# A triangular inverse by doubling: the level mask put on the product by VectorE, instead of on the matrix by GpSimd

## The chip, the cores and the metric

The kernel runs on one core of one Trainium2 chip. The metric is the time of one execution on the device in microseconds. Five engines work side by side and wait for each other by semaphores: TensorE (PE in the profile; PEld is its loading of weights), VectorE (DVE), ScalarE (ACT), GpSimd (POOL) and SyncE (SP), which issues the DMAs. Matrix products go to PSUM, all other tiles are in SBUF.

## What is computed

One layer over 1024 tokens of width 1024: an RMS norm, one input projection, two mixers side by side (a pooling group and a gated delta rule with four heads), an output projection, a squared-ReLU MLP of width 4096, a final norm. What the change touches is inside the delta rule, where for each chunk of tokens and each head a unit lower triangular system is solved:

```python
    kb = kh * beta[..., None]
    m = jnp.einsum('bhncd,bhnjd->bhncj', kb, kh) * decay_strict
    lhs = jnp.eye(C, dtype=f32) + m
    rhs = jnp.concatenate([vh * beta[..., None], kb * jnp.exp(gcum)[..., None]], axis=-1)
    sol = lax.linalg.triangular_solve(lhs, rhs, left_side=True, lower=True)
```

The kernel takes chunks of 128 tokens, eight in all, and forms the inverse of `lhs` for all four heads of a chunk at a time.

## The kernel before

The tokens are done in two halves of 512. `dense()` is the main thread of TensorE: for each half the projections to k, q, v, z and the pooling input, each in two blocks of 256 columns, then the output projection. Full-precision products are made of three fp32r products of a high and a low part. The parts of the weights come from `split_w` (L125): a load into `raw`, a ScalarE copy to the high part (L132), and a subtraction for the low part `wl` (L133), on VectorE or on GpSimd as the caller says: GpSimd for the k weights of the first half and for all of the second half. A projection to q, k or v ends in `conv_silu` (L378), where VectorE adds three convolution taps to `cy` (L391); the pooling input goes to `pool_group` (L395), a ladder of VectorE additions and small copies `nxt` (L409, L410).

Beside this run "strands", generators that put their instructions between the matmuls of `dense()`. For each chunk `c` there are `prepare` (L510), `query` (L554), `invert` (L573), `correct` (L605) and `scan` (L636). TensorE's order is written out: a counter of matmul time decides which strand puts its next piece after which matmul, and a strand says with `yield` how much TensorE time it leaves before its next piece (`SLACK` is 2.0 us). The orders of VectorE, ScalarE and GpSimd are made by a scheduler when the kernel is built. Each engine works through its order strictly in turn.

`prepare` makes the normalised keys: GpSimd raises the sums of squares `rk` to the power -1/2 (L152), VectorE multiplies (`kn`, L533). Then it makes `m1`, the f16 matrix of all four heads with the identity added (L550), with its rounding rest in `m2` (L549, GpSimd), and GpSimd makes `dec`, `ds` and `kd` (L525, L527, L540). `invert` doubles the size of the inverted diagonal blocks six times, from 2 to 128. `t` is the inverse so far, `tt` its transpose. Before the loop VectorE masks `m1` to the first level (`bl`, L578) and adds the identity (`tt`, L579). In each of the six rounds:

- GpSimd masks `m1` with the constant matrix `lev[l]`, which is -1 in the blocks of that level and 0 elsewhere, into the f16 tile `bl` (L588), one instruction of 128x512 for all heads; `bl` has two buffers.
- TensorE forms the product `px` of `bl` and `t` (L590), four matmuls of 128x128, into a PSUM bank.
- VectorE adds the identity and writes the f16 tile `xx` (L592).
- After 2 us of TensorE time, TensorE forms `tt` times `xx` and `xx` times `tt`, and ScalarE copies both to the new `t` and `tt` (L598, L599).

The seven matrices `lev[l]` are made once at the start by GpSimd (L255 to L260), between its first weight splits.

Of the kernel before, what the change touches and what calls it, by code (L numbers as in the profile page):

```python
# [10 lines left out]
F16 = mybir.dt.float16  # L11
AF = mybir.ActivationFunctionType
ALU = mybir.AluOpType
PSUM = bass.MemoryType.PSUM

P = 128
# [12 lines left out]
def hybrid_trunk(ctx, tc, x, norm_mix, w_in, conv_w, w_pool, pool_scale, a_log, dt_bias,  # L29
                 gdn_norm, w_out, norm_mlp, w_up, w_down, norm_final, out):  # L30
    nc = tc.nc
    V, A, G, T = nc.vector, nc.scalar, nc.gpsimd, nc.tensor
# [54 lines left out]
    ident = const.tile([P, P], F32, name="ident")  # L87
# [153 lines left out]
    ident_h = gp.tile([P, P], F16, name="ident_h")  # L241
# [4 lines left out]
    upto_r = gp.tile([P, P], F32R, name="upto_r")  # L246
    V.tensor_copy(upto_r, upto)

    lev = []
    for l in range(7):  # L250
        b = 1 << l
        m = gp.tile([P, P], F16, name=f"lev{l}")
        nb = P // (2 * b)
        m3 = m.rearrange("p (n q) -> p n q", q=2 * b)
        G.memset(m3[:, :, 0:b], 0.0)  # L255
        G.memset(m3[:, :, b:2 * b], -1.0)

        G.affine_select(m3, m3, pattern=[[-2 * b, nb], [0, 2 * b]], compare_op=ALU.is_ge, fill=0.0, base=0,
                        channel_multiplier=1)
        G.affine_select(m3, m3, pattern=[[2 * b, nb], [0, 2 * b]], compare_op=ALU.is_gt, fill=0.0, base=b,  # L260
                        channel_multiplier=-1)
        lev.append(m)

    cnt_i = gp.tile([P, 16], mybir.dt.int32, name="cnt_i")
# [14 lines left out]
    def done(name, after=0.0):  # L279
        flags[name] = T.now + after  # L280
# [198 lines left out]
    def bc(m):  # L479
        return m.unsqueeze(1).broadcast_to(hs)  # L480
# [7 lines left out]
    def gt(nm, bufs=1, dt=F32, shape=hs, tag=None):  # L488
        return gp.tile(shape, dt, name=nm, tag=tag or nm, bufs=bufs)

    def bank():
        return work_bank().rearrange("p (h c) -> p h c", h=NH)

    def mm(acc, lhsT, rhs, start=True, stop=True):
        for h in range(NH):
            T.matmul(acc[:, h, :], lhsT[:, h, :], rhs[:, h, :], start=start, stop=stop)
# [76 lines left out]
    def invert(c, r):  # L573

        m1 = r["m1"]
        t, tt = gt("t", 3, F16), gt("tt", 3, F16)
        b0 = gt("bl", 2, F16)
        V.tensor_tensor(b0, m1, bc(lev[0]), op=ALU.mult)  # L578
        V.tensor_tensor(tt, b0, bc(ident_h), op=ALU.add)  # L579
        yield 1.0 * SLACK  # L580
        pt = bank()
        for h in range(NH):
            T.matmul(pt[:, h, :], tt[:, h, :], ident_h, start=True, stop=True)
        A.copy(t, pt)
        yield 0.9 * SLACK
        for l in range(1, 7):
            bl = gt("bl", 2, F16)
            G.tensor_tensor(bl, m1, bc(lev[l]), op=ALU.mult)  # L588
            px = bank()
            mm(px, bl, t)  # L590
            xx = gt("xx", dt=F16)
            V.tensor_tensor(xx, px, bc(ident), op=ALU.add)  # L592
            yield 1.0 * SLACK
            pt, ptt = bank(), bank()
            mm(pt, tt, xx)
            mm(ptt, xx, tt)
            t, tt = gt("t", 3, F16), gt("tt", 3, F16)
            A.copy(t, pt)  # L598
            A.copy(tt, ptt)  # L599
            if l < 6:  # L600
                yield 1.0 * SLACK
        r.update(t=t, tt=tt)
        done(f"inverted{c}", 1.0 * SLACK)
# [103 lines left out]
    def inverts():  # L707
        for c in range(NT):
            yield f"prepared{c}"
            yield from invert(c, made[c])  # L710
# [308 lines left out]
    first = {}  # L1019
# [168 lines left out]
```

## Time and profile before

| | |
|---|---|
| median of 3 runs | 1172.87 us (1172.27 to 1178.7) |
| the profiled execution | 1173.46 us, its span in the trace 1171.7 us |
| 0 to 455 us: both halves' projections, with the delta rule beside them | PE busy 415.16, DVE 354.29, ACT 276.09, POOL 214.74 us |
| 455 to 600 us: the rest of the output projection, into the MLP | PE busy 126.50, DVE 96.99, ACT 75.35, POOL 43.53 us |
| 600 us to the end: the MLP and the final norm | PE busy 558.18, DVE 335.27, ACT 251.33, POOL 68.82 us |
| the six masks of a round on GpSimd, L588 | 48 instructions, 62.0 us, 79.9 to 440.6 us |
| the identity added to the product on VectorE, L592 | 48 instructions, 32.8 us |

The profile is of one execution. A row of the timeline has the start, the time taken, the engine, the line, the operation and the tiles as out<-in; in brackets stands how long the engine had been idle before it and what ended that. A row of the waits has the engine that waited, what it waited for, the total in us, the number of times, and the longest. A row of a line's instructions has min/median/max in ns.

### The profile page before, as it was taken

How to read it: one execution, taken by the hardware profiler on the slowest of the kernel's cores; microseconds unless marked ns; L12 is line 12 of the kernel's file. 1: busy time of each engine (PE TensorE's matmuls, PEld its weight loads, DVE VectorE, ACT ScalarE, POOL GpSimd, SP SyncE). 2: the span in 40 equal slices, each digit the busy share in tenths (PEclk: the TensorE clock that was granted, in tenths of full speed). 3: DMA queues.
4: the chain of work that ended last, by engine and by line, in shares of the span. 5: the costliest groups of instructions: out<-in, count | busy, mean ns of one | idle time of the engine just before them, and what ended most of it. 6: DMA issues, size and time to landing. Idle time of an engine off the chain costs nothing.

```text
span 1171.7 us, 15587 instructions
## 1 busy us (share of the span) xinstructions
PE 1099.8 (94%) x5606; PEld 893.7 (76%) x5606; DVE 786.6 (67%) x1224; ACT 602.8 (51%) x1117; POOL 327.1 (28%) x288
## 2 busy tenths in 40 slices
PE   6998999988898999995999999999979999999997
PEld 5777777767687788773788888888868888888886
DVE  5698698878879775559646454545455597465584
ACT  6666566566565554635545454545443333334353
POOL 7033365465754431045132323131100000000010
PEclk9999999999999999997999999999989999999999
DMA  5233211111213321121344444444298797256561
GB/s 161 81 101 116 61 52 41 55 55 43 66 41 126 109 72 37 37 72 54 133 155 153 147 150 152 145 153 145 81 361 294 262 394 242 90 195 192 189 215 72
DMA packets 93047, 155.23 MB, mean 132 GB/s; under 512 B 7781, under 2 KB 45738, under 8 KB 92970
## 3 DMA queue, kind: packets, MB, share of 16 engines
q1 hardware_dynamic: 92970, 154.24, 39.1%
q8 instruction: 44, 0.72, 0.2%
q14 instruction: 33, 0.27, 0.1%
HBM read 120.66 MB, written 33.55 MB: 132 GB/s over the span
## 4 chain that ended last, share of the span: by engine, by line
PE 71%; DVE 12%; ACT 3%; issue 2%; POOL 2%; DMA 0%; POOLq 0%; DVEq 0%; ACTq 0%; SPq 0%
PE bank L44 53%; PE acc L44 17%; DVE cy L391 2%; DVE tl L927 1%; DVE nxt L410 1%; DVE xx L592 1%; PE bank L48 1%; DVE nxt L409 0%; DMA x<-hd 0%; DVE r L918 0%; ACT th L172 0%; DVE ul L173 0%; DVE ml L764 0%; DVE m L546 0%; DVE kn L533 0%
## 5 line engine op out<-in xcount | busy, mean ns | idle before, releaser
L44 PE MATMUL bank<-th,wh 128*128 128x512 f32 x448 | 178.3, 398 | 11.7 <-ACT th L926 10.7
L44 PE MATMUL bank<-tl,wh 128*128 128x512 f32 x448 | 178.1, 398 | 3.0 <-DVE tl L927 2.9
L44 PE MATMUL bank<-th,wl 128*128 128x512 f32 x448 | 177.5, 396 | 2.2 <-DVE wl L933 2.2
L932 ACT CAST sh<-x 128x1024 fp32r<-128x1024 f32 x55 | 57.9, 1054 | 160.9 <-PE bank L44 154.2
L44 PE MATMUL bank<-th,sh 128*128 128x512 f32 x344 | 133.8, 389 | 0.0
L44 PE MATMUL bank<-th,sl 128*128 128x512 f32 x344 | 133.8, 389 | 0.0
L44 PE MATMUL bank<-tl,sh 128*128 128x512 f32 x344 | 133.8, 389 | 0.0
L44 PE MATMUL acc<-uh,wh 128*128 128x512 f32 x320 | 130.4, 407 | 1.1 <-DVE ul L173 0.6
L44 PE MATMUL acc<-ul,wh 128*128 128x512 f32 x320 | 129.3, 404 | 0.0
L932 ACT CAST wh<-wu 128x512 fp32r<-128x512 f32 x112 | 69.1, 621 | 116.0 <-PE bank L44 98.2
L44 PE MATMUL acc<-uh,wl 128*128 128x512 f32 x320 | 128.8, 402 | 0.0
L933 DVE TENSOR_TENSOR sl<-x,sh 128x1024 fp32r<-128x1024 f32 x55 | 67.3, 1223 | 88.1 <-ACT sh L932 88.0
L933 DVE TENSOR_TENSOR wl<-wu,wh 128x512 fp32r<-128x512 f32 x112 | 80.4, 722 | 45.0 <-ACT wh L932 45.0
L44 PEld LDWEIGHTS bank<-th,wh 128*128 128x128 f32 x448 | 85.1, 190 | 32.0 <-ACT th L926 11.4
L44 PEld LDWEIGHTS bank<-tl,wh 128*128 128x128 f32 x448 | 85.0, 190 | 24.5 <-DVE tl L927 5.4
L44 PEld LDWEIGHTS bank<-th,wl 128*128 128x128 f32 x448 | 85.1, 190 | 22.3 <-DVE wl L933 3.1
L152 POOL TENSOR_TENSOR stf<-stf,mhalf 128x1 f32<-128x1 f32 x8 | 7.9, 998 | 329.7 <-DVE stf L1125 329.7
L588 POOL TENSOR_TENSOR bl<-m,lev 128x512 f16<-128x512 f16 x48 | 62.0, 1291 | 82.5 <-PE bank L44 70.2
L391 DVE SCALAR_TENSOR_TENSOR cy<-cr,cols,cy 128x512 f32<-128x512 f32 x72 | 74.1, 1034 | 8.2 <-ACT cy L389 7.7
L133 POOL TENSOR_TENSOR wl<-raw,wh 128x512 fp32r<-128x512 f32 x48 | 68.0, 1421 | 36.4 <-ACT wh L132 36.2
L44 PEld LDWEIGHTS bank<-th,sl 128*128 128x128 f32 x344 | 64.6, 188 | 13.5
L44 PEld LDWEIGHTS bank<-th,sh 128*128 128x128 f32 x344 | 64.6, 188 | 13.5
(325 smaller groups left out, 2372.1 us busy)
## 6 DMA issues: line engine op xcount, KB each, us to landing
w<-in_w_down_dram SPq DMA_DIRECT2D x72, 512.0 KB, 6.9
x<-hd SPq DMA_DIRECT2D x56, 512.0 KB, 3.3
raw<-in_w_in_dram SPq DMA_DIRECT2D x80, 256.0 KB, 2.7
wu<-in_w_up_dram SPq DMA_DIRECT2D x16, 1024.0 KB, 5.4
hd<-s SPq DMA_DIRECT2D x48, 256.0 KB, 2.0
hd<-u SPq DMA_DIRECT2D x32, 256.0 KB, 2.1
raw<-in_w_out_dram SPq DMA_DIRECT2D x24, 256.0 KB, 2.8
xin<-in_x_dram SPq DMA_DIRECT2D x8, 512.0 KB, 5.1
```

Source lines behind the costliest of these rows:

```text
L44: T0.matmul(out, lhsT, rhs, start=start, stop=stop, skip_group_check=goes_on)
L48: T0.transpose(out, in_, identity)
L133: eng.tensor_tensor(lo, raw, hi.bitcast(F32), op=ALU.subtract)
L152: last["rsqrt"] = G.tensor_tensor(s, s, mhalf[:, :n], op=ALU.pow)
L391: V.scalar_tensor_tensor(cy, cr[:, e:e + HALF], tap[e], cy, op0=ALU.mult, op1=ALU.add)
L410: V.tensor_tensor(nxt[:, n:], cur[:, n:], cur[:, :W - n], op=ALU.add)
L588: G.tensor_tensor(bl, m1, bc(lev[l]), op=ALU.mult)
L592: V.tensor_tensor(xx, px, bc(ident), op=ALU.add)
L927: V.tensor_tensor(TL[i][:, j, :], block(r, j), TH[i][:, j, :].bitcast(F32), op=ALU.subtract)
L932: A.copy(hi, src)
L933: V.tensor_tensor(lo, src, hi.bitcast(F32), op=ALU.subtract)
```

## The change

The mask moves from the matrix to the product. Since the mask only selects blocks of the result of `px`, the product of the whole `m1` with `t` can be masked after it. The diagonal of that product is 1 (both factors are unit triangular), so a mask that is 1 on the diagonal puts the identity there as well, and no addition is left. The constants `lev[l]` for l > 0 are laid out transposed and get a diagonal of ones by a third AFFINE_SELECT each; `lev[0]` gets the diagonal too, and `tt` comes of one product.

```diff
@@ in the constants
-        G.memset(m3[:, :, 0:b], 0.0)
-        G.memset(m3[:, :, b:2 * b], -1.0)
-
-        G.affine_select(m3, m3, pattern=[[-2 * b, nb], [0, 2 * b]], compare_op=ALU.is_ge, fill=0.0, base=0,
+        first = l > 0
+        G.memset(m3[:, :, 0:b], -1.0 if first else 0.0)
+        G.memset(m3[:, :, b:2 * b], 0.0 if first else -1.0)
+
+        o = b if first else 0
+        G.affine_select(m3, m3, pattern=[[-2 * b, nb], [0, 2 * b]], compare_op=ALU.is_ge, fill=0.0, base=-o,
                         channel_multiplier=1)
-        G.affine_select(m3, m3, pattern=[[2 * b, nb], [0, 2 * b]], compare_op=ALU.is_gt, fill=0.0, base=b,
+        G.affine_select(m3, m3, pattern=[[2 * b, nb], [0, 2 * b]], compare_op=ALU.is_gt, fill=0.0, base=o + b,
                         channel_multiplier=-1)
+
+        G.affine_select(m, m, pattern=[[-1, P]], compare_op=ALU.not_equal, fill=1.0, base=0, channel_multiplier=1)
         lev.append(m)
@@ invert
-        b0 = gt("bl", 2, F16)
-        V.tensor_tensor(b0, m1, bc(lev[0]), op=ALU.mult)
-        V.tensor_tensor(tt, b0, bc(ident_h), op=ALU.add)
+        V.tensor_tensor(tt, m1, bc(lev[0]), op=ALU.mult)
...
         for l in range(1, 7):
-            bl = gt("bl", 2, F16)
-            G.tensor_tensor(bl, m1, bc(lev[l]), op=ALU.mult)
             px = bank()
-            mm(px, bl, t)
+            mm(px, m1, t)
             xx = gt("xx", dt=F16)
-            V.tensor_tensor(xx, px, bc(ident), op=ALU.add)
+            V.tensor_tensor(xx, px, bc(lev[l]), op=ALU.mult)
```

TensorE's order stays the same, with `m1` as the weights of 192 matmuls where `bl` was. The orders that the scheduler makes change. Lines behind the constants have numbers up to 5 higher in the changed kernel.

VectorE at the first inverse, from the finished `m1` (here `m_816`) to the first `xx`, before:

```order
L550 TENSOR_TENSOR m_816<-m_816,ident_h 128x512
L386 COPY chalo<-cr 128x3
L578 TENSOR_TENSOR bl<-m_816,lev_239 128x512
L391 SCALAR_TENSOR_TENSOR cy<-cr,cols,cy 128x512
L579 TENSOR_TENSOR tt<-bl,ident_h 128x512
L133 TENSOR_TENSOR wl<-raw,wh 128x512
L391 SCALAR_TENSOR_TENSOR cy<-cr,cols,cy 128x512
```

The same place now (`m1` is `m_837`):

```order
L555 TENSOR_TENSOR m_837<-m_837,ident_h 128x512
L391 COPY chalo<-cr 128x3
L584 TENSOR_TENSOR tt<-m_837,lev_239 128x512
L396 SCALAR_TENSOR_TENSOR cy<-cr,cols,cy 128x512
L133 TENSOR_TENSOR wl<-raw,wh 128x512
L396 SCALAR_TENSOR_TENSOR cy<-cr,cols,cy 128x512
```

`bl` is gone, and `tt` stands ahead of the convolution tap that it followed.

GpSimd where the trace of before has 192 to 205 us, from the power of one chunk's output sums (`so`, L152) through the last mask of an inverse to the `kd` of the next chunk, before:

```order
L152 TENSOR_TENSOR so<-so,mhalf 128x4
L525 TENSOR_TENSOR dec<-dec,upto 128x512
L588 TENSOR_TENSOR bl<-m_1817,lev_269 128x512
L133 TENSOR_TENSOR wl<-raw,wh 128x512
L527 TENSOR_TENSOR ds<-dec,ident 128x512
L152 TENSOR_TENSOR rk<-rk,mhalf 128x4
L756 TENSOR_TENSOR qT<-qT,zT 128x4x128
L133 TENSOR_TENSOR wl<-raw,wh 128x512
L540 TENSOR_TENSOR kd<-kn,kds_526 128x512
```

Now:

```order
L152 TENSOR_TENSOR so<-so,mhalf 128x4
L530 TENSOR_TENSOR dec<-dec,upto 128x512
L133 TENSOR_TENSOR wl<-raw,wh 128x512
L532 TENSOR_TENSOR ds<-dec,ident 128x512
L152 TENSOR_TENSOR rk<-rk,mhalf 128x4
L759 TENSOR_TENSOR qT<-qT,zT 128x4x128
L545 TENSOR_TENSOR kd<-kn,kds_547 128x512
```

The mask is gone from the front of `rk`, and a weight split has moved from ahead of `kd` to behind it.

VectorE at the same time, from one `xx` of that inverse to the next and the `kn` of the next chunk, before:

```order
L592 TENSOR_TENSOR xx<-bank,ident 128x512
L530 TENSOR_SCALAR rk<-rk 128x4
L391 SCALAR_TENSOR_TENSOR cy<-cr,cols,cy 128x512
L592 TENSOR_TENSOR xx<-bank,ident 128x512
L533 TENSOR_TENSOR kn<-bank,rk 128x512
```

Now:

```order
L595 TENSOR_TENSOR xx<-bank,lev_271 128x512
L535 TENSOR_SCALAR rk<-rk 128x4
L538 TENSOR_TENSOR kn<-bank,rk 128x512
L396 SCALAR_TENSOR_TENSOR cy<-cr,cols,cy 128x512
L595 TENSOR_TENSOR xx<-bank,lev_279 128x512
```

`kn`, which takes the `rk` that GpSimd has worked on, stands ahead of a tap and of the second `xx`. In three other chunks it moves ahead of other work in the same way.

## The prediction

> **What bounds the kernel now.** I read the busy shares of the page first, then the busy times by stretch, then who waits for whom.
>
> ```profile
> PE 1099.8 (94%) x5606; PEld 893.7 (76%) x5606; DVE 786.6 (67%) x1224; ACT 602.8 (51%) x1117; POOL 327.1 (28%) x288
> ...
> 75.00:455.00 380.00, 350.62 (x2299) 283.52 (x2298) 302.08 (x562) 229.17 (x524) 188.07 (x144) 0.99 0.23 71
> ```
>
> PE is busy for 94% of the span. The second line is the stretch from 75 to 455 us, in which the inverses run beside the projections (its columns: length, busy time of PE, PEld, DVE, ACT, POOL, granted clock, DMA share, GB/s). PE is busy for 350.62 of 380 us. PE's order is written by hand and the change leaves it alone, so nothing but PE's idle time in this stretch, 29.4 us, and matmuls at a lower clock can be won here. Who ends that idle time:
>
> ```profile
> POOL bl L588 <- PE bank L44: 70.2, 20, 7.9
> ...
> PE bank L44 <- DVE xx L592: 15.1, 10, 3.0
> PE bank L48 <- DVE kn L533: 2.9, 2, 1.5
> PE acc L44 <- DVE wol L133: 2.9, 1, 2.9
> PE bank L44 <- DVE nxt L409: 1.7, 1, 1.7
> ...
> PE bank L48 <- DVE on L679: 0.8, 1, 0.8
> ```
>
> PE hardly ever waits for GpSimd's masked matrices: GpSimd waits 70.2 us for PE before it makes them. PE waits for **VectorE**: 15.1 + 2.9 + 2.9 + 1.7 + 0.8, and 0.7 for tt, shown below, are 24.1 us (waits under 0.8 us are left out). So the removal of bl is worth nothing as a shorter path. It is worth what GpSimd does to VectorE meanwhile:
>
> ```profile
> L391 DVE SCALAR_TENSOR_TENSOR cy<-cr,cols,cy x72: 734/752/1846, 27.2 to 313.4; 128x512 f32<-128x512 f32 x72
> L592 DVE TENSOR_TENSOR xx<-bank,ident x48: 673/682/693, 89.5 to 451.3; 128x512 f16<-128x512 f32 x48
> ```
>
> (min/median/max in ns.) The convolution tap, with two inputs in SBUF, takes 752 ns as a rule and up to 1846; xx, with one input in PSUM, never over 693. The long ones stand beside GpSimd instructions, as the next rows show.
>
> **The change part by part.** *First place, the first inverse.* VectorE, then GpSimd, then PE:
>
> ```profile
> 79.81 0.42 DVE L578 TENSOR_TENSOR bl<-m,lev 128x512 f16<-128x512 f16 x1
> 80.15 1.65 DVE L391 SCALAR_TENSOR_TENSOR cy<-cr,cols,cy 128x512 f32<-128x512 f32 x1
> ...
> 82.67 1.63 DVE L391 SCALAR_TENSOR_TENSOR cy<-cr,cols,cy 128x512 f32<-128x512 f32 x1
> ...
> 84.90 2.31 DVE L391 SCALAR_TENSOR_TENSOR cy<-cr,cols,cy 128x512 f32<-128x512 f32 x2
> 79.86 1.40 POOL L588 TENSOR_TENSOR bl<-m,lev 128x512 f16<-128x512 f16 x1 [0.54 <-DVE chalo L386]
> 82.22 1.54 POOL L588 TENSOR_TENSOR bl<-m,lev 128x512 f16<-128x512 f16 x1 [0.96 <-DVE tt L579]
> 85.06 1.61 POOL L588 TENSOR_TENSOR bl<-m,lev 128x512 f16<-128x512 f16 x1 [1.30 <-PE bank L44]
> 82.20 0.40 PE L44 MATMUL bank<-ident_h,tt 128*128 128x128 f16 x4 [0.74 <-DVE tt L579]
> 90.25 0.52 PE L44 MATMUL bank<-xx,tt 128*128 128x128 f16 x4 [2.97 <-DVE xx L592]
> ```
>
> Three times a bl runs and the tap beside it ends with it: 1.65 - 0.75 = 0.90, 1.63 - 0.75 = 0.88 and 2.31 - 2 x 0.75 = 0.81 us. With bl gone these 2.59 us go, and the 0.42 us of L578, whose work (mask, then identity) is one product now. So tt takes the place of L578 at 79.81, ahead of the tap, and PE's 0.74 us go; xx, behind the same taps and the same `at` as before, comes about 3.0 us earlier, and PE, itself 0.74 us earlier, finds it some 0.7 us late instead of 2.97. Of 3.71 us, 3.0 go.
>
> *Second place, a middle inverse:*
>
> ```profile
> 367.51 1.27 DVE L764 TENSOR_TENSOR ml<-pT,mh 128x512 fp32r<-128x512 f32 x1
> ...
> 370.83 0.68 DVE L764 TENSOR_TENSOR ml<-pT,mh 128x512 fp32r<-128x512 f32 x1
> 371.43 1.65 DVE L764 TENSOR_TENSOR ml<-qT,mh 128x512 fp32r<-128x512 f32 x1
> 367.06 1.17 POOL L588 TENSOR_TENSOR bl<-m,lev 128x512 f16<-128x512 f16 x1 [0.36 <-DVE tt L579]
> ...
> 371.12 1.41 POOL L588 TENSOR_TENSOR bl<-m,lev 128x512 f16<-128x512 f16 x1 [0.77 <-PE bank L44]
> 375.44 0.40 PE L44 MATMUL bank<-xx,tt 128*128 128x128 f16 x4 [1.43 <-DVE xx L592]
> ```
>
> Against the unhindered 0.68 us of a split, 0.59 + 0.97 us are lost beside bl, and an L578 goes too (0.42): more than the 1.43 us that PE waits. All 1.43 go.
>
> *Third place, where no bl is near:*
>
> ```profile
> 356.79 1.25 DVE L409 COPY nxt<-nxt 128x4 f32<-128x4 f32 x1
> 356.71 1.30 POOL L133 TENSOR_TENSOR wl<-raw,wh 128x512 fp32r<-128x512 f32 x1 [1.81 <-ACT wh L132]
> 361.04 0.38 PE L44 MATMUL bank<-xx,tt 128*128 128x128 f16 x4 [2.50 <-DVE xx L592]
> ```
>
> Here a copy of four columns takes 1.25 us beside one of GpSimd's weight splits, and the splits stay. Nothing of the 2.50 us goes.
>
> Together the three places hold 3.71 + 1.43 + 2.50 = 7.64 us of waits, and 3.0 + 1.43 = 4.43 go: 58%. I carry that share over to all: 0.58 x 24.1 = 14.0 us. Where PE stops waiting it meets the next VectorE result sooner; I let a third come back as new waits, a choice between none and half, and keep 9.3 us. Against that third also stands a change of order: at one place xx comes behind a third tap where it had two ahead of it, at 0.75 us unless the queue is empty.
>
> *The clock.* Windows of 4 us, granted clock third from the end:
>
> ```profile
> 90.00:94.00 4.00, 3.75 (x16) 3.07 (x16) 2.21 (x5) 2.11 (x4) 0.00 (x0) 0.57 0.68 268
> 322.00:326.00 4.00, 4.00 (x21) 3.55 (x22) 2.18 (x7) 1.63 (x3) 1.16 (x1) 0.57 0.00 0
> 362.00:366.00 4.00, 4.00 (x25) 3.09 (x24) 3.97 (x10) 3.89 (x10) 1.87 (x2) 1.00 0.94 360
> ```
>
> Twice the clock falls after a pause, at (1 - 0.57) x 4 = 1.7 us each; after the 2.50 us pause at 358 it does not. The first fall follows the 2.97 us wait, which I expect gone: 1.7 us more. The other I leave. The Trainium skill (TensorE: Matmul & The Clock Gate, Why this matters for your kernels) warns only of idle gaps above about 3 us; by that the pause of 2.97 us would cost nothing, the term would be nought and the time 1.7 us longer. The rows show the drop, and decide.
>
> *The prices of the instructions.*
>
> ```profile
> L588 POOL TENSOR_TENSOR bl<-m,lev 128x512 f16<-128x512 f16 x48 | 62.0, 1291 | 82.5 <-PE bank L44 70.2
> L619 DVE TENSOR_TENSOR hh<-bank,tt x8: 673/680/692, 129.1 to 459.5; 128x512 f16<-128x512 f32 x8
> L579 DVE TENSOR_TENSOR tt<-bl,ident_h x8: 409/411/1269, 81.7 to 416.0; 128x512 f16<-128x512 f16 x8
> L260 POOL TENSOR_SCALAR_AFFINE_SELECT lev<-lev x7: 294/400/704, 18.7 to 25.9; 128x128 f16<-128x128 f16 x7
> 26.59 3.00 POOL L133 TENSOR_TENSOR wl<-raw,wh 128x512 fp32r<-128x512 f32 x2 [0.38 <-ACT wh L132]
> ```
>
> The 48 xx multiply a PSUM bank by an f16 mask where they added an f32 identity. The nearest row is hh, a PSUM bank with an f16 tile: 680 ns against 682, so nothing; at worst 48 x (693 - 682) ns = 0.5 us, at best 0.4 the other way. The new tt is an f16 product as L578 is: 0.41 us, and up to 1.27 beside GpSimd. The seven added AFFINE_SELECT cost GpSimd 7 x 0.40 = 2.8 us (2.1 to 4.9). They go among the first weight splits, of which the last ends at 29.59; they are hidden by the weights that PE still has, since no wait of PE is ended by GpSimd, and I cost them at nothing. If that cover failed, the last two splits would be up to 4.9 us late. The dense m1 in the place of bl as PE's weights changes no count of loads or matmuls: nothing.
>
> The sum: 9.3 + 1.7 = 11.0 us off the profiled execution's own 1173.46 us gives **1162 us**; the median of the runs shown, 1172.87, is 0.6 us lower.
>
> **The rivals.** *The collisions only move.* GpSimd's splits, no longer queued behind bl, start earlier and hold VectorE elsewhere, as at 358. For it: they and the other GpSimd work are 188.07 - 62.0 = 126 us of the stretch. Against it: nothing refills the 62. The Trainium skill (SBUF — State Buffer, Who interferes with whom) says that of a VectorE instruction with two SBUF inputs and a GpSimd instruction that reads SBUF, the second blocks until the first ends; the rows at 80 to 85 us agree (0.81 to 0.90 us each). By that rule alone bl could hold VectorE for up to 62.0 us, far over what PE waits, and as many collisions as splits would remain. Time if nine tenths come back: 0.1 x 14.0 = 1.4 us, 1172 us; with the noise 1168 to 1174.
>
> *Full relief.* VectorE's load falls, from 302.08 of 380 us, so far that its queue empties between inverses: three quarters of the 24.1 us and both falls of the clock go, 18.1 + 3.4 = 21.5 us: 1152 us.
>
> *Slower: kn ahead of its turn.* In the new VectorE order kn, which waits for GpSimd's rk, stands in four chunks ahead of work that it followed, once ahead of a tap and of xx:
>
> ```profile
> 196.61 1.17 POOL L588 TENSOR_TENSOR bl<-m,lev 128x512 f16<-128x512 f16 x1
> ...
> 200.22 1.01 POOL L152 TENSOR_TENSOR rk<-rk,mhalf 128x4 f32<-128x4 f32 x1
> 200.72 0.75 DVE L391 SCALAR_TENSOR_TENSOR cy<-cr,cols,cy 128x512 f32<-128x512 f32 x1 [2.92 <-ACT cy L389]
> ```
>
> VectorE's queue is in order, so tap and xx wait behind kn. Without bl, rk ends at about 201.23 - 1.17 = 200.06, before the tap could start at 200.72: free. Should rk end after that, each of the four places costs up to rk and a split ahead of it, about 1.0 + 1.3 = 2.3 us, 9 us in all, and if the relief above fails too the time is 1182 us. It decides from rk later than the tap.
>
> *The change not doing what it says* is out: in the new order of GpSimd no bl is left.
>
> **How the numbers follow.** Forecast 0.58 (1156 with no give-back and the second fall of the clock gone too: 14.0 + 3.4 = 17.4 us; 1166 with half of the 14.0 given back and no fall gone), full relief 0.12, moved collisions 0.23, slower 0.07. Half a per cent, 5.9 us, is about what a measurement of this kernel tells from no change. Faster has forecast and full relief, 0.70; same 0.23; slower 0.07. The range, 1151 to 1173, takes in full relief and the moved collisions and leaves out the slower case and the edges.
>
> **What would show it.** PE's waits for xx in the inverse stretch down from 15.1 to 6 to 8 us; the tap's mean there, with stretched ones only beside splits; the wait at 87 us under 1 us and the clock at 1.00 behind it; the wait at 358 still there; xx at 0.68 us; no PE wait before 50 us that GpSimd ends. I am wrong if VectorE's busy time falls by 25 us or so and PE's waits do not, or if a wait for kn grows.

## The result, and the profile after

| | before | after |
|---|---|---|
| median | 1172.59 us (1172.27 to 1178.7, 4 runs) | 1155.43 us (1154.56 to 1156.41, 4 runs) |
| the profiled execution | 1173.46 us, span 1171.7 us | 1154.56 us, span 1152.9 us |
| mean granted clock of TensorE | 0.984 | 0.987 |

The ratio of the two is 0.9842, with a 95% interval of 0.9818 to 0.9865: 1.6% faster, 17.2 us by the medians. The time is 6.6 us under the forecast 1162 and inside the range.

To see where the 18.8 us between the two spans lie, the same piece of TensorE's program is cut out of both traces. It begins at 75 us and ends at the first transposition of the MLP's input `xn`, which both traces have 2440 matmuls later. The window of before, then that of after (length, busy time of PE, PEld, DVE, ACT, POOL, granted clock, DMA share, GB/s):

```profile
75.00:480.16 405.16, 375.79 (x2440) 304.65 (x2439) 313.42 (x587) 236.91 (x543) 190.19 (x147) 0.99 0.22 67
```

```profile
75.00:462.55 387.55, 371.67 (x2440) 302.56 (x2439) 285.88 (x579) 236.13 (x543) 128.82 (x99) 0.99 0.24 72
```

The piece is 17.6 us shorter; the remaining 1.2 us lie behind it. PE's idle time, length less busy time, fell from 29.4 to 15.9 us: **13.5 us**. Its busy time fell by 4.1 us, and a part of that is the clock, shown below. GpSimd lost 61.4 us and VectorE 27.5 us of busy time. Only about 3.4 us of VectorE's are instructions that are gone (eight of 0.42 us); in the other 24 us the instructions that stayed took less time. The rows below trace that to holds: an instruction is held when it takes longer than alone because a GpSimd instruction is running.

PE's waits in that piece after the change (who waited for what, total, times, longest):

```profile
PE bank L44 <- DVE xx L595: 3.3, 6, 0.8
PE acc L44 <- DVE wol L133: 3.0, 2, 1.9
PE bank L48 <- DVE kn L538: 2.7, 2, 1.4
PE bank L44 <- DVE ee L617: 1.6, 2, 0.9
PE bank L44 <- ACT t L601: 1.6, 3, 1.0
PE bank L44 <- ACT qT L397: 1.5, 1, 1.5
PE bank L44 <- ACT ph L433: 1.1, 1, 1.1
PE bank L48 <- DVE on L682: 0.4, 1, 0.4
```

Of the six waits for VectorE that the forecast summed to 24.1 us, 3.3 + 3.0 + 2.7 + 0.4 = 9.4 are left; those for `nxt` and `tt` are gone. That is 14.7 us, 61%. Against it stand 0.9 us more for `ee`, 0.8 us more for ScalarE's `ph`, 0.4 us more for ScalarE's `t` and `vT`, and 1.5 us for ScalarE's `qT`, a new wait: 3.6 us. Waits of before that the sum had left out are gone too: `y` (1.0 us), `ul` (0.8) and `zT` (0.3).

The two instructions of VectorE that were shown before, now (min/median/max in ns):

```profile
L396 DVE SCALAR_TENSOR_TENSOR cy<-cr,cols,cy x72: 736/746/1872, 27.6 to 300.3; 128x512 f32<-128x512 f32 x72
...
L595 DVE TENSOR_TENSOR xx<-bank,lev x48: 673/684/692, 86.4 to 433.7; 128x512 f16<-128x512 f32 x48
```

The tap's group in 75 to 455 us of the changed kernel (count, then busy us and mean ns), and the same group before:

```profile
L396 DVE SCALAR_TENSOR_TENSOR cy<-cr,cols,cy 128x512 f32<-128x512 f32 x48 | 44.1, 921 | 4.1 <-ACT cy L394 3.6
```

```profile
L391 DVE SCALAR_TENSOR_TENSOR cy<-cr,cols,cy 128x512 f32<-128x512 f32 x48 | 53.9, 1127 | 6.7 <-ACT cy L389 6.3
```

The product costs what the addition did, 684 ns against 682. The tap's mean fell from 1127 to 921 ns, while its longest in this stretch is 1767 ns against 1846 (the 1872 above lies ahead of 75 us): there are fewer collisions, and those that are left are about as long.

The first of the three places of the prediction, after the change; VectorE, then PE, and GpSimd has no row between 79.3 and 90 us:

```profile
79.75 0.42 DVE L584 TENSOR_TENSOR tt<-m,lev 128x512 f16<-128x512 f16 x1
80.09 0.74 DVE L396 SCALAR_TENSOR_TENSOR cy<-cr,cols,cy 128x512 f32<-128x512 f32 x1
...
82.62 0.74 DVE L396 SCALAR_TENSOR_TENSOR cy<-cr,cols,cy 128x512 f32<-128x512 f32 x1
...
86.40 0.68 DVE L595 TENSOR_TENSOR xx<-bank,lev 128x512 f16<-128x512 f32 x1
...
87.13 0.38 PE L44 MATMUL bank<-xx,tt 128*128 128x128 f16 x4 [0.84 <-DVE xx L595]
```

No tap is stretched; PE does not wait for `tt` at all, and 0.84 us for `xx` where it waited 2.97.

The third place, where the forecast left the whole wait of 2.50 us. Before, a second copy was stretched beside the next split, behind the copy at 356.79 that the prediction shows:

```profile
358.67 1.11 DVE L409 COPY nxt<-nxt 128x8 f32<-128x8 f32 x1
358.38 1.38 POOL L133 TENSOR_TENSOR wl<-raw,wh 128x512 fp32r<-128x512 f32 x1 [0.38 <-ACT wh L132]
```

The same place in the changed kernel:

```profile
340.69 1.14 DVE L414 COPY nxt<-nxt 128x8 f32<-128x8 f32 x1
341.74 0.69 DVE L415 TENSOR_TENSOR nxt<-nxt 128x520 f32<-128x520 f32 x1
342.35 0.68 DVE L595 TENSOR_TENSOR xx<-bank,lev 128x512 f16<-128x512 f32 x1
340.49 1.32 POOL L133 TENSOR_TENSOR wl<-raw,wh 128x512 fp32r<-128x512 f32 x1 [3.26 <-ACT wh L132]
342.12 1.44 POOL L133 TENSOR_TENSOR wl<-raw,wh 128x512 fp32r<-128x512 f32 x1 [0.32 <-ACT wh L132]
343.08 0.38 PE L44 MATMUL bank<-xx,tt 128*128 128x128 f16 x4 [0.81 <-DVE xx L595]
```

The two splits are still there, and so is the collision, but one copy is stretched where two were: when the second split begins, at 342.12, VectorE is already at the last addition of the ladder, and the next instruction is `xx`. Its one tensor input of that size is in PSUM; it takes 0.68 us beside the split, so it is not held.

The clock, in windows of 4 us (it stands third from the end of a row), after the change:

```profile
87.00:91.00 4.00, 3.87 (x28) 3.24 (x28) 2.61 (x6) 3.45 (x9) 0.71 (x1) 1.00 0.91 329
...
380.00:384.00 4.00, 2.40 (x10) 1.61 (x11) 3.61 (x7) 0.92 (x2) 1.89 (x2) 0.71 0.24 79
384.00:388.00 4.00, 4.00 (x19) 3.34 (x18) 1.95 (x4) 1.73 (x4) 0.91 (x1) 0.50 0.38 122
```

And before, at the corresponding place of the output projection:

```profile
400.00:404.00 4.00, 3.60 (x12) 2.83 (x13) 3.37 (x7) 1.39 (x3) 1.76 (x2) 0.62 0.36 131
404.00:408.00 4.00, 4.00 (x27) 3.16 (x26) 2.19 (x4) 1.56 (x3) 1.04 (x1) 0.95 0.20 70
```

The falls at 90 and at 322 us are both gone: after the change no window of 4 us between 64 and 380 us is under 1.00. A third one, at 401 us, which the forecast had not listed, has become twice as long. Over the whole span the clock cost (1 - 0.984) x 1171.7 = 18.7 us before and (1 - 0.987) x 1152.9 = 15.0 us after, 3.7 us less.

### The profile page after: what moved, and what is told of

The parts are those of the page before. It is cut to its first block, busy times and chain, and to the rows that moved or that the text cites. A ratio compares the mean times of both kernels' runs of the same rounds, so it can differ in the third digit from the quotient of the medians.

```text
span 1152.9 us, 15516 instructions
## 1 busy us (share of the span) xinstructions
PE 1094.7 (95%) x5606; PEld 890.2 (77%) x5606; DVE 760.5 (66%) x1216; ACT 601.5 (52%) x1117; POOL 267.3 (23%) x247
## 4 chain that ended last, share of the span: by engine, by line
PE 73%; DVE 9%; ACT 3%; POOL 2%; issue 2%; DMA 1%; POOLq 0%; DVEq 0%; SPq 0%; ACTq 0%
PE bank L44 54%; PE acc L44 18%; DVE cy L396 2%; DVE tl L930 1%; PE bank L48 1%; POOL rk L152 1%; DVE xx L595 0%; DMA x<-hd 0%; ACT th L172 0%; DVE r L921 0%; POOL wl L133 0%; DVE nxt L415 0%; DVE wl L936 0%; DVE m L551 0%; POOL wu L955 0%
## 5 line engine op out<-in xcount | busy, mean ns | idle before, releaser
L44 PE MATMUL bank<-th,wh 128*128 128x512 f32 x448 | 178.2, 398 | 11.5 <-ACT th L929 10.5
L44 PEld LDWEIGHTS bank<-th,wh 128*128 128x128 f32 x448 | 85.1, 190 | 31.8 <-ACT th L929 11.2
L152 POOL TENSOR_TENSOR stf<-stf,mhalf 128x1 f32<-128x1 f32 x8 | 7.9, 998 | 329.1 <-DVE stf L1128 329.1
L44 PEld LDWEIGHTS bank<-th,sl 128*128 128x128 f32 x344 | 64.6, 188 | 13.5
L44 PEld LDWEIGHTS bank<-tl,sh 128*128 128x128 f32 x344 | 64.6, 188 | 13.5
L44 PEld LDWEIGHTS acc<-uh,wh 128*128 128x128 f32 x320 | 60.3, 188 | 13.6 <-ACT cy L394 1.9
```

Of the source, the lines that this page charges most:

```text
L44: T0.matmul(out, lhsT, rhs, start=start, stop=stop, skip_group_check=goes_on)
L152: last["rsqrt"] = G.tensor_tensor(s, s, mhalf[:, :n], op=ALU.pow)
```

## The experiments

Three theories of where the gain came from. **A**: a GpSimd instruction that reads SBUF holds VectorE, and PE waits for VectorE. **B**: the path is shorter and VectorE has fewer instructions. **C**: GpSimd's queue is shorter, so its other results come sooner. In the table each stretch begins at 75 us and ends at the first transposition of `xn`; "idle" is its length less PE's busy time, from the windows of the profiled execution. The ratios are to runs of the kernel before made together with each experiment, whose medians were 1172.99 to 1174.25 us; so a difference of a microsecond or so between two medians of the table says nothing.

| kernel | median us | ratio to before [95%] | stretch | PE idle | VectorE busy |
|---|---|---|---|---|---|
| before | 1172.59 | | 405.2 | 29.4 | 313.4 |
| after | 1155.43 | 0.9842 [0.9818, 0.9865] | 387.6 | 15.9 | 285.9 |
| e1_reader | 1173.6 | 1.0002 [0.9988, 1.0016] | 403.7 | 27.5 | 308.8 |
| e2_readers | 1192.03 | 1.0155 [1.0128, 1.0181] | 423.9 | 39.7 | 329.9 |
| e3_queue_only | 1158.43 | 0.9868 [0.9846, 0.989] | 389.2 | 15.2 | 284.5 |
| e4_tt_only | 1169.11 | 0.9969 [0.9955, 0.9983] | 405.2 | 27.2 | 308.0 |
| e5_splits_vector | 1150.18 | 0.9799 [0.9779, 0.982] | 383.0 | 11.2 | 283.8 |
| e6_mask_vector | 1164.39 | 0.9929 [0.9903, 0.9956] | 396.8 | 20.0 | 308.8 |
| e7_copies | 1161.04 | 0.9896 [0.9879, 0.9914] | 392.5 | 18.2 | 291.7 |
| e8_masks_ahead | 1177.49 | 1.0027 [1.0013, 1.004] | 410.1 | 31.2 | 310.0 |
| e9_little_gpsimd | 1144.05 | 0.9743 [0.9721, 0.9765] | 375.8 | 7.2 | 289.2 |

**Giving the products back to GpSimd, for nobody.** The changed kernel, with a GpSimd product in each round whose result nothing reads:

```diff
         for l in range(1, 7):
+            bl = gt("bl", 2, F16)
+            G.tensor_tensor(bl, t, bc(lev[l]), op=ALU.mult)
             px = bank()
             mm(px, m1, t)
```

> The changed kernel with one GpSimd product more in each of the six rounds of an inverse, t times the level mask, 128x512 in f16, into a tile that nothing reads: 48 in all, as many and of the same shape as the bl that the change removed, and nothing on TensorE or VectorE waits for them. Theory A (GpSimd instructions that read SBUF hold VectorE): most of the gain of 17.2 us is lost, 1166 to 1174 us, and VectorE's waits-ended-at-PE for xx rise from 3.3 to 10 us or more. Theory B (the gain is the shorter path to px, or the eight fewer VectorE instructions): 1154 to 1159 us.

It took 1173.6 us: 48 instructions that nobody waits for took back the whole gain. B would have had none of that. The timeline of the first inverse shows how (GpSimd, VectorE, PE):

```profile
82.53 1.36 POOL L593 TENSOR_TENSOR bl<-t,lev 128x512 f16<-128x512 f16 x1 [3.10 <-ACT t L589]
...
82.80 1.64 DVE L396 SCALAR_TENSOR_TENSOR cy<-cr,cols,cy 128x512 f32<-128x512 f32 x1
...
88.20 0.38 PE L44 MATMUL bank<-xx,tt 128*128 128x128 f16 x4 [1.73 <-DVE xx L597]
```

One tap is stretched by 0.90 us (1.64 against 0.74 at 82.62 in the changed kernel), `xx` comes later by as much, and PE's wait for it grows from 0.84 to 1.73 us, by 0.89. In the list of PE's waits those for `xx` are back at 12.1 us:

```profile
PE bank L44 <- DVE xx L597: 12.1, 9, 4.3
```

**Twice as many.** Two such products a round, 96 in all.

```diff
+            for _ in range(2):
+                bl = gt("bl", 2, F16)
+                G.tensor_tensor(bl, t, bc(lev[l]), op=ALU.mult)
```

> As the run with one added GpSimd product, but with two per round, 96 in all. Theory A: each adds as much hold as the first, so slower than the kernel before, 1178 to 1195 us. Theory B: 1154 to 1162 us.

1192.03 us: the first 48 cost 18.2 us, the second 18.4. In the stretch of the table idle time rose by 11.6 and then by 12.2 us, for 23 and 21 us more of VectorE's busy time, with not one more instruction on VectorE. The clock added to it, at 0.96 in this stretch against 0.99: PE's busy time for the same matmuls is 384.19 us, 12.5 more than after the change. The window of e2:

```profile
75.00:498.86 423.86, 384.19 (x2441) 310.57 (x2439) 329.94 (x579) 236.48 (x543) 258.09 (x195) 0.96 0.21 64
```

**GpSimd kept busy, without reading.** A power of four columns in the place of the product: it takes GpSimd nearly as long, but there is hardly anything to read.

```diff
+            po = gt("po", 2, F32, shape=[P, NH])
+            G.tensor_tensor(po, t[:, 0, 0:NH], mhalf, op=ALU.pow)
```

> The changed kernel with 48 GpSimd powers of 128x4 elements, of about 1.0 us each, at the same places as the added products: they take GpSimd's time, but read 8 elements per partition where the product reads 1024. Theory A, that it is the reading that holds VectorE: 1154 to 1160 us. Theory C, that it is GpSimd's queue (rk, kd and the weight splits come later behind anything that takes GpSimd's time): as slow as with the products, 1165 to 1174 us.

The group of the powers (busy us, mean ns):

```profile
L593 POOL TENSOR_TENSOR po<-t,mhalf 128x4 f32<-128x4 f16 x48 | 54.6, 1137 | 105.9 <-ACT t L603 72.2 <-ACT t L589 21.8 <-PE bank L44 5.9
```

The first of them, and the tap that begins while it runs:

```profile
82.29 1.16 POOL L593 TENSOR_TENSOR po<-t,mhalf 128x4 f32<-128x4 f16 x1 [3.17 <-ACT t L589]
...
82.49 0.75 DVE L396 SCALAR_TENSOR_TENSOR cy<-cr,cols,cy 128x512 f32<-128x512 f32 x1
```

The tap is not stretched, where the product of e1 held it by 0.90 us. And the window of the stretch:

```profile
75.00:464.21 389.21, 373.97 (x2440) 304.31 (x2439) 284.53 (x579) 236.54 (x543) 181.01 (x147) 0.98 0.24 71
```

54.6 us of GpSimd's time cost 3.0 us, and neither VectorE's busy time nor PE's idle time grew (284.5 and 15.2 us against 285.9 and 15.9). PE's busy time did, by 2.3 us, with more falls of the clock (one is shown at the end). So GpSimd's queue (C) is worth little of the gain; what costs is how much a GpSimd instruction moves in SBUF. The power reads and writes four columns where the product reads and writes 512, and no run separates the reading from the writing.

**The shorter start of the inverse alone.** The kernel before, with `tt` as one product; the masks of the rounds stay on GpSimd.

```diff
+        if l == 0:
+            G.affine_select(m, m, pattern=[[-1, P]], compare_op=ALU.not_equal, fill=1.0, base=0, channel_multiplier=1)
...
-        b0 = gt("bl", 2, F16)
-        V.tensor_tensor(b0, m1, bc(lev[0]), op=ALU.mult)
-        V.tensor_tensor(tt, b0, bc(ident_h), op=ALU.add)
+        V.tensor_tensor(tt, m1, bc(lev[0]), op=ALU.mult)
```

> The kernel before with only the first level changed: lev[0] has the diagonal and tt is one product of m1, so that eight VectorE instructions of 0.42 us and more go; the 48 masks stay on GpSimd. Theory A: 1169 to 1173 us, 1 to 3 us of the 17. Theory B in its form of fewer VectorE instructions: 1156 to 1165 us.

1169.11 us, at the low end of A's range. It is 0.3% faster, 2 to 5 us by the interval: a small part of the 17.2. PE's idle time in its profile is 27.2 us, 2.2 less than before. Its profiled execution, 1172.58 us, was the slowest of its ten, so its windows say little beyond that.

**A reader with one input.** In the place of e1's product a copy of `t`.

```diff
+            bl = gt("bl", 2, F16)
+            G.tensor_copy(bl, t)
```

> The changed kernel with 48 GpSimd copies t to an unread tile, 128x512 f16, one input instead of two, at the places of the 48 products that gave 1173.6 us. Theory A1 (any GpSimd instruction that works on SBUF holds VectorE for as long as it runs): the loss is 18.2 us times the ratio of the copy's duration to the product's 1.32 us; with a copy of 0.5 to 1.0 us that is 7 to 14 us, 1162 to 1169 us, and VectorE's taps beside copies are stretched to the copy's end. Theory A2 (only GpSimd instructions with two SBUF inputs hold it): 1155 to 1159 us, with VectorE's taps beside copies at 0.75 us.

The group of the copies (busy us, mean ns):

```profile
L593 POOL COPY bl<-t 128x512 f16<-128x512 f16 x48 | 36.5, 759 | 111.2 <-ACT t L603 89.0 <-ACT t L589 21.9
```

The timeline at the first inverse, GpSimd and then VectorE:

```profile
82.26 0.83 POOL L593 COPY bl<-t 128x512 f16<-128x512 f16 x1 [3.09 <-ACT t L589]
...
82.53 1.10 DVE L396 SCALAR_TENSOR_TENSOR cy<-cr,cols,cy 128x512 f32<-128x512 f32 x1
```

1161.04 us, 5.6 more than without the copies and between both expectations. A copy holds the tap too, by 0.36 us (1.10 against 0.74), where the product at the same place held it by 0.90. In both cases the tap ends 0.54 to 0.55 us after GpSimd's instruction (83.63 and 83.09; 84.44 and 83.89), so the two inputs are not needed for it. A price in proportion to the hold, 18.2 x 0.36 / 0.90 = 7.3 us, comes nearer to the 5.6 than one in proportion to the duration, 18.2 x 0.76 / 1.32 = 10.5 us. Over the whole stretch VectorE's busy time rose by 5.8 us, against 23.0 for the products, which gives 18.2 x 5.8 / 23.0 = 4.6 us. The Trainium skill (SBUF — State Buffer, Who interferes with whom) says that whoever comes first keeps the shared pair of ports for its whole instruction and the other blocks. The rows of the product and the copy agree but for 0.2 us: a tap that takes 0.74 us alone ends 0.54 to 0.55 us behind GpSimd's instruction. The power of e3 does not agree: it reads four columns of SBUF and runs for 1.16 us, and the tap that begins beside it takes 0.75 us; there the measurement decides.

**The same masks, made by VectorE.** The kernel before, with one letter changed: the mask stays on the matrix.

```diff
-            G.tensor_tensor(bl, m1, bc(lev[l]), op=ALU.mult)
+            V.tensor_tensor(bl, m1, bc(lev[l]), op=ALU.mult)
```

> The kernel before with the six masked matrices of an inverse made by VectorE (0.41 us each, 48 of them, 19.7 us) instead of GpSimd; the mask stays on the matrix. Theory A (VectorE's time counts, whether its own or held): 24.7 us of holds beside the masks go and 19.7 us of own work come, so most of the gain is not there: 1164 to 1172 us, VectorE busy in 75 to 455 us at 294 to 304 us. Rival D (GpSimd's masks cost through GpSimd alone, its queue and its memory traffic, and own VectorE work of this size is free): 1154 to 1160 us, as the changed kernel.

The group of the masks on VectorE (busy us, mean ns):

```profile
L588 DVE TENSOR_TENSOR bl<-m,lev 128x512 f16<-128x512 f16 x48 | 25.8, 539 | 0.1
```

And from the list of PE's waits:

```profile
PE bank L44 <- DVE xx L592: 2.2, 5, 0.8
```

1164.39 us, at the edge of A's range: half of the change's gain comes with taking the masks off GpSimd, and by subtraction the other half with not needing them at all (and with the shorter `tt`). What A did not say is in the table: VectorE is as busy as with e1's readers (308.8 us in both), yet PE is idle for 20.0 us against 27.5. In this pair a microsecond of VectorE's own work costs less than one in which it is held.

**The masks at another time.** The masks of before run on GpSimd as soon as PE has freed a buffer, just when VectorE is due to make `xx`. Does that timing make them dear? In this kernel they are issued ahead of the rounds, in four buffers.

```diff
-        b0 = gt("bl", 2, F16)
+        b0 = gt("bl", 4, F16)
...
+        bls = [gt("bl", 4, F16) for _ in range(6)]
+        for l in range(1, 7):
+            G.tensor_tensor(bls[l - 1], m1, bc(lev[l]), op=ALU.mult)
...
-            bl = gt("bl", 2, F16)
-            G.tensor_tensor(bl, m1, bc(lev[l]), op=ALU.mult)
             px = bank()
-            mm(px, bl, t)
+            mm(px, bls[l - 1], t)
```

> The kernel before with the same 48 masked matrices on GpSimd, but issued ahead of the rounds of an inverse, in four buffers instead of two: they no longer start each at the moment when PE has finished px and VectorE is due to make xx. Theory H (what a hold costs depends on when it falls: a mask that starts when px ends holds the work that stands just ahead of xx): 1160 to 1168 us, PE's waits for xx in 60 to 470 us down from 15.1 to 5 to 10 us, with GpSimd's busy time in 75 to 455 us still 180 to 190 us. Rival I (only the amount of held VectorE time counts): 1170 to 1175 us, waits for xx at 13 to 16 us.

From the list of PE's waits:

```profile
PE bank L44 <- DVE xx L593: 10.7, 8, 4.0
...
PE bank L44 <- DVE nxt L409: 2.6, 1, 2.6
PE bank L44 <- DVE ee L615: 2.3, 3, 0.8
PE bank L44 <- DVE tt L579: 2.1, 2, 1.7
```

1177.49 us, slower than before: theory H falls, and the time lies above I's range too. The waits for `xx` did fall, from 15.1 to 10.7 us, between the two expectations, but those for `nxt`, `tt` and `ee` grew from 1.7, 0.7 and 0.7 us to 2.6, 2.1 and 2.3. The wait for `tt` grew because the first masks now run while VectorE makes `tt`: L579 takes 1034 ns at the median where it took 411. The masks were moved only in part, since an inverse fills seven tiles `bl` and there are four buffers: GpSimd still waits 36.5 us for PE before it makes them, where it waited 70.2. So this other placement is no cheaper; that no placement would be is not shown.

**More off GpSimd.** If holds are what costs, GpSimd's other readers are worth moving too. First the 40 weight splits of the second half, `project(1, ...)`, from GpSimd to VectorE:

```diff
-        yield from project(1, "k", G)
+        yield from project(1, "k", V)
...
-        yield from project(1, "q", G)
-        yield from project(1, "v", G)
-        yield from project(1, "p", G)
-        yield from project(1, "z", G, conv_done)
+        yield from project(1, "q", V)
+        yield from project(1, "v", V)
+        yield from project(1, "p", V)
+        yield from project(1, "z", V, conv_done)
```

> The changed kernel with the weight splits of the second half (k, q, v, pooling input, z) on VectorE instead of GpSimd. Theory A (what counts is VectorE's time, its own work and its holds together): a split costs VectorE 0.68 us of its own, and a GpSimd split holds it by about as much (some 27 us over 40 splits by the stretched VectorE instructions of the changed kernel), so about no change: 1151 to 1159 us, with GpSimd's busy time in 75 to 455 us below 90 us and VectorE's busy time there within 6 us of 283.54. Rival B2 (VectorE's own work is dearer than holds, since the holds fall where VectorE has slack): 1162 to 1172 us, with more waits of PE for xx and for wl.

The window of the stretch:

```profile
75.00:458.02 383.02, 371.80 (x2440) 303.27 (x2439) 283.75 (x619) 236.73 (x543) 71.56 (x59) 0.99 0.25 73
```

1150.18 us, faster than both kernels and just under A's range. VectorE does 40 instructions more and is busy for 283.75 us where it was for 285.88: their own time took the place of holds. Part of the gain seems to have another cause, GpSimd's queue (C). In the changed kernel PE's waits for `kn` hang on GpSimd's `rk`, as here:

```profile
290.79 0.69 DVE L538 TENSOR_TENSOR kn<-bank,rk 128x512 f32<-128x512 f32 x1 [1.61 <-POOL rk L152]
...
291.63 0.63 PE L48 MATMUL bank<-ident,kn 128*128 128x128 f32 x4 [1.28 <-DVE kn L538]
```

With the splits off GpSimd these waits fall from 2.7 to 0.2 us, over half of the 4.7 us that PE's idle time fell by. Then also `dec`, `ds`, `kd`, `m2` and the output gate, all 128x512 in size:

```diff
-        G.tensor_tensor(dec, dec, bc(upto), op=ALU.mult)
+        V.tensor_tensor(dec, dec, bc(upto), op=ALU.mult)
...
-        G.tensor_tensor(ds, dec, bc(ident), op=ALU.subtract)
+        V.tensor_tensor(ds, dec, bc(ident), op=ALU.subtract)
...
-        G.tensor_tensor(kd, kn, bcol(kds), op=ALU.mult)
+        V.tensor_tensor(kd, kn, bcol(kds), op=ALU.mult)
...
-        G.tensor_tensor(m2, m, m1, op=ALU.subtract)
+        V.tensor_tensor(m2, m, m1, op=ALU.subtract)
...
-        G.tensor_tensor(o, o, zT[i][:, :, cs:cs + P], op=ALU.mult)
+        V.tensor_tensor(o, o, zT[i][:, :, cs:cs + P], op=ALU.mult)
```

> The changed kernel with the splits of the second half on VectorE, as in the run that took 1150.18 us, and also the two decay matrices, the scaled keys, the rest of m1 and the output gate on VectorE instead of GpSimd, 40 more instructions. GpSimd is left with the powers and the first block's splits. Theory A (VectorE's own 0.68 us and the hold are about alike, and own work is placed where VectorE has time): 1145 to 1151 us, VectorE busy in 75 to 455 us at 280 to 295 us, GpSimd under 30 us. Rival B2 (VectorE's queue becomes the bound): 1153 to 1165 us, with waits of PE for xx, kn and the matrices m back above 10 us.

The tap in 75 to 455 us (min/median/max in ns), in the changed kernel and then in this one:

```profile
L396 DVE SCALAR_TENSOR_TENSOR cy<-cr,cols,cy x48: 736/745/1767, 80.1 to 300.3; 128x512 f32<-128x512 f32 x48
```

```profile
L396 DVE SCALAR_TENSOR_TENSOR cy<-cr,cols,cy x48: 743/747/754, 78.8 to 293.8; 128x512 f32<-128x512 f32 x48
```

And the window of the stretch:

```profile
75.00:450.78 375.78, 368.58 (x2440) 300.97 (x2439) 289.23 (x650) 236.14 (x542) 22.83 (x23) 1.00 0.25 74
```

1144.05 us, just under A's range, 2.6% under before and 1.0% under the changed kernel. In this stretch no tap is stretched any more: the longest takes 754 ns, where it took 1767. Ahead of 75 us, where GpSimd still makes splits, taps of up to 1870 ns remain. VectorE is busier than after the change (289.2 against 285.9 us), and still PE's idle time has fallen to 7.2 us. B2, VectorE as the bound, is not in sight.

## Why the prediction was right, and what it sized wrongly

**What bounds the kernel: right.** PE's order and its 2440 matmuls in the stretch stayed, and the gain is 13.5 us of PE's idle time, 4.1 us of its busy time and 1.2 us behind the stretch, 18.8 us together. That the masks were worth what GpSimd does to VectorE, and nothing as a path, is shown by e1: instructions outside every path bring the old time back.

**The share of 58%, 14.0 us: right in size, and partly by luck.** Of the 24.1 us of waits 14.7 went. At the first place 0.84 us are left where 0.7 were forecast; at the second PE no longer waits. The third place was read wrongly: not all of its 2.50 us stayed, but 0.81, since the splits that hold the ladder fell at another moment. So 6.0 of the 7.64 us of the three places went, 78%. Other waits of the sum went less than 58% (`kn` 2.9 to 2.7, `wol` 2.9 to 3.0), which happened to make up for it. Both waits for `kn` that are left stand behind a wait of VectorE for GpSimd's `rk`, of 0.69 and 1.61 us, which is no hold.

**"I let a third come back as new waits": this term was mis-sized.** It took 4.7 us off the gain. PE's idle time fell by 13.5 us, all but 0.5 of the 14.0, so next to nothing came back on balance. New and longer waits did come, 3.6 us in all, but waits that the sum had left out went as well, 2.1 us (`y`, `ul`, `zT`), and the sum itself lost 14.7 us and not 14.0. The experiments show no floor that would give waits back: e7, e1 and e2 find PE's idle time following the time in which VectorE is held, by 2.3 us for 5.8, 11.6 for 23.0 and 23.8 for 44.1, and in e5 and e9 it falls further, to 7.2 us.

**The clock, 1.7 us: half of what it was.** Two falls in the stretch went instead of one, the one of the output projection grew by one, and the MLP has one less: 3.7 us by the mean clocks. Without the give-back and with both falls gone the forecast's own terms give 14.0 + 3.4 = 17.4 us and 1156 us, beside the measured 1155.43; that the clock's part fits so well is luck, since the fall that grew and the one that went in the MLP were not foreseen and cancel. Some 2 us of PE's busy time in the stretch are not accounted for by the clock: 4.1 less one fall of 1.7; no run was made for them.

**What would show it.** The waits for `xx` fell to 3.3 us, lower than the 6 to 8 forecast. The clock behind the first place is at 1.00. The price of `xx` and the 0.42 us of `tt` are as forecast. The seven AFFINE_SELECT stayed hidden; no wait of PE before 60 us is ended by GpSimd. One sign failed: the wait at 358 us was to stay, and 0.81 us of it did.

**Two readings.** The prediction says that the tap ends with the `bl` beside it; by its own rows the tap ends 0.54 us later, at all three places (81.80 against 81.26, 84.30 against 83.76, 87.21 against 86.67). Its sums of lost time hold, since they go by the taps' own durations. And the waits for `ul`, 0.8 us, belong in the 24.1 us by the rule that it gives.

**The rivals.** Collisions that only move (1172 us): the splits do collide still, the tap's longest in the stretch is 1767 ns, but they did not multiply. It is right that moved collisions can be as dear, as e8 shows for one placement; here they were removed. The slower case, `kn` ahead of its turn, cost PE nothing: its waits for `kn` are 2.7 us against 2.9. VectorE does stand waiting for `rk` longer than before, 6.6 us against 1.2 in the piece from 75 us. At the place shown in the prediction that was free: `kn` begins at 190.87, and the tap behind it needs a ScalarE result that ends at 191.40. Full relief (1152 us) came nearest among the rivals.

**What stays open.** Why a microsecond of VectorE's own work costs PE less than a held one (e6 against e1, 4.1 us of idle time against 11.6 for 23 us each). The order of VectorE is made with the own work in it and cannot know of the holds, which would explain it; that was argued, not tried. In e5 and e9 the share of GpSimd's shorter queue was not separated from that of the holds. Only one other timing of the holds was tried (e8), and it was no better.

## What to carry to other kernels

An engine that nobody waits for can still be the one to unload: look for one and the same VectorE instruction with a median of 0.75 us and a maximum of 1.85, and see which GpSimd rows stand beside the long ones. Here, with VectorE on PE's path, 40 elementwise instructions of 128x512 on GpSimd cost VectorE as much time as doing them itself (285.9 us busy against 283.8 in e5). Such work is better folded into an instruction that reads PSUM, or tried on VectorE; leave to GpSimd what reads little. And where a wait is removed by taking away its cause, rather than by moving it, don't discount the gain for new waits without a row that shows where they would come from.

## What the runs showed of the hardware

- A GpSimd power of four columns takes 1.14 us, as long as many a product of 128x512, and VectorE's busy time does not grow with it (e3). A copy of 128x512 with a single input does hold VectorE (e7).
- A held tap ended 0.54 to 0.55 us behind the GpSimd instruction that held it, at all five places shown: three before the change, one in e1, one in e7. So the hold is what is left of GpSimd's instruction when the tap begins, less 0.2 us.
- The length of a pause of PE alone does not decide whether the granted clock falls behind it. In e3 it fell after a pause of 2.01 us; before the change it did not fall after 2.50 us. In e3 it also fell to 0.57 at 184 to 188 us, behind pauses of 1.05 and 0.23 us; in the changed kernel the same two pauses are 1.07 and 0.23 us long, and the clock behind them stays at 1.00. The windows of e3, with the pause at 341.7 to 343.7 us:

```profile
340.00:344.00 4.00, 1.99 (x14) 1.48 (x14) 3.93 (x7) 0.63 (x1) 4.00 (x3) 1.00 0.40 91
344.00:348.00 4.00, 4.00 (x16) 2.85 (x13) 4.00 (x10) 3.15 (x8) 1.36 (x2) 0.59 0.75 237
```

That fall costs (1 - 0.59) x 4 = 1.6 us. The Trainium skill (TensorE: Matmul & The Clock Gate, Why this matters for your kernels) warns of gaps above about 3 us; here a fall comes after 2.01 us, and the measurement decides. A pause of 1 to 2 us can therefore cost more than its own length, and many of them add up: e2's busy time for the same matmuls is 12.5 us over that of the changed kernel.
